# Convolution LayerNorm on VectorE, deferred steps in a woven stream, an early bias table and w2 in 22 loads: one encoder layer on eight cores

## The chip, the cores and the metric

The kernel runs on the 8 cores of one Trainium2 chip, one batch element to a core, with no traffic between cores. The metric is the device time of the slowest core in microseconds (us). The program gives each of a core's five engines a list of its own: PE (matmul), VectorE (DVE in the profile), ScalarE (ACT), GpSimd (POOL) and SP, which here only issues DMAs. In the trace of the kernel before, an instruction that waits holds up what stands behind it in its list: VectorE stood 29.2 us before the copy L423, and the eviction L322, listed after it, came only at 84.3 us. Some executions fall into a second, slower state, in which the cores of a die show a lower granted clock: in the changed kernel's run of 1262.65 us one die shows 0.818 to 0.832 (1252.7 to 1261.1 us), the other 0.973 to 0.978 (1091.8 to 1100.5 us). The medians quoted are those of fast runs alone. Ratios are the mean time of one kernel's fast runs over that of the other's fast runs of the same rounds, so they are not quite the ratio of the medians.

## The reference, cut to what matters

```python
proj = x @ w_in            # conv GLU input | q | k | v | memory q | three branch gates
y_conv = conformer_conv(glu_in, ...)        # GLU -> depthwise conv, width 31 -> LayerNorm -> swish -> projection
y_attn = windowed_gqa(q, k, v, rel_bias, sink) @ w_attn_out     # +-128 tokens, bias by relative position
y_mem  = memory_attention(q_mem, mem, w_mem_kv) @ w_mem_out
gates  = sigmoid(gate_logits + b_gate)
merged = gates[0] * y_conv + gates[1] * y_attn + gates[2] * y_mem
x = layer_norm(ALPHA * x + merged @ w_o, ln1_g, ln1_b)
gate, up = split(x @ w_ffn_in)
return layer_norm(ALPHA * x + (silu(gate) * up) @ w_ffn_out, ln2_g, ln2_b)
```

A core has 2048 tokens of width 1024; the convolution has 512 channels, the FFN 2816.

## The kernel before

The program is one stream per engine. "Main" work (projections) is interleaved with "side" work (convolution, window attention, memory attention) by weight:

```python
def weave(mains, sides):
    ...
    for w, f in mains:
        f()
        mc += w
        while sides and sc + sides[0][0] / 2 <= stot * mc / mt:
            sw, sf = sides.pop(0)
            sf()
            sc += sw
```

The convolution is cut into 16 groups: 4 blocks of 512 tokens by 4 sets of 128 channels. The program's matmuls read each group's input shifted by 0 to 3 tokens and laid out over the partitions. SP makes such a window with 16 small transfers, into one of three buffers:

```python
for j in range(4):
    for r in range(4):
        lo = 32 + 512 * k - 15 + r
        uq_tok[i] = dma(sp, UQ[r3][j][32 * r:32 * r + 32, 0:540],
                        U0[32 * j:32 * j + 32, c, lo:lo + 540], uq_slot[r3], deps)
```

The LayerNorm and swish that end a block run mostly on GpSimd, each step issued as soon as the program reaches it:

```python
def fin(c):
    t_z1 = pool.run(... cvs[c] * rstdb ...)
    ...
    t_th = act.run(... tanh(scale * cvs[c] + bias) ...)
    t_z2 = pool.run(... cvs[c] * gamma/2 + beta/2 ...)
    t_sT[k, c] = dve.run(... (th2[r] + 1) * cvs[c] ...)
```

The bias table of the window attention is made between the first projections, goes to HBM and comes back reversed in three SP loads. The FFN's first weights are cast once into a cache in HBM (`w_bf_cache`, 22 tiles) and read back four times. Its second weights, w2, come in two large loads when the FFN starts.

The softmax here doesn't subtract the row's maximum and nothing guards it: scores larger than these inputs give would overflow.

Of the kernel before, what the change touches and what calls it, by code (L numbers as in the profile page):

```python
# [11 lines left out]
D = 1024  # L12
# [78 lines left out]
def _build(plan):  # L91
# [162 lines left out]
    geb = V(149, [8, 512])  # L254
    Brev = V(155.75, [128, 3, 8, 128])

# [37 lines left out]
    t_pads = pool.run(lambda: nc.gpsimd.memset(U0[:, :, T + 32:UW], 0.0))  # L294
    t_wq = load(wq, w_q_d)
    t_wkv = load(wkv, w_kv_d)
    t_wqm = load(wqm, w_qm_d)
    t_memt = load(memT, memt_d)
    t_wmk = [load(wmk[:, i], w_mkv_d[:, i]) for i in range(2)]
    load_xt(2)  # L300
    load_xt(3)
    t_vones = pool.run(lambda: nc.gpsimd.memset(vaug[:, :, :, 64:65], 1.0))
# [12 lines left out]

    ev = {"i": 0}

    def evac(dst, src, deps):
        ev["i"] += 1
        if ev["i"] % 2:  # L320
            return act.run(lambda: nc.scalar.copy(dst, src), deps)  # L321
        return dve.run(lambda: nc.vector.tensor_copy(dst, src), deps)  # L322
# [13 lines left out]
    def g_gate(k, c):  # L336
        b, tk = group8(lambda kc: wglu[:, c, 1, kc, :], lambda kc: xT[:, k, kc, :], k, [t_glu[c]])
        r = gst["i"] % 3
        gst["i"] += 1
        t = act.run(lambda: nc.scalar.activation(th2[r], ps[:, b, :], AF.Tanh, scale=0.5), [tk, th_free[r]])  # L340
        banks.release(b, t)
        gpend[k, c] = (r, t)
# [58 lines left out]
    def setup_bias():  # L401
        b, dd = banks.alloc(1)
        t_g = mm(ps[0:8, b, :], rb33[:], oh, True, True, [t_small, dd], inc=True)
        t_b0 = act.run(lambda: nc.scalar.activation(ge, ps[0:8, b, :], AF.Exp), [t_g])
        banks.release(b, t_b0)
        t_b1 = dve.run(lambda: nc.vector.tensor_tensor(out=geb, in0=ge, in1=rv, op=ALU.mult), [t_b0, t_small])
        btab["st"] = load(gexp_d.ap(), geb, [t_b1], sp)
        s_mt = new_slot("mt")
        for kb in range(3):
            btab["rev"] = dma(sp, Brev[:, kb, :, :], bass.AP(gexp_d, kb * 128, [[1, 128], [512, 8], [1, 128]]),  # L410
                              s_mt, [btab["st"]])

# [7 lines left out]
    def setup_rev():  # L420
        for kb in range(3):
            src = bass.AP(Brev.tensor, Brev[:, kb, 0, 127:128].offset, [[Brev.ap[0][0], 128], [128, 8], [-1, 128]])
            btab["t"] = dve.run(lambda: nc.vector.tensor_copy(expB[:, kb, :, :], src), [btab["rev"]])  # L423

    uq_slot = [new_slot("uq") for _ in range(3)]
# [35 lines left out]
    def conv_steps(k):  # L461
# [3 lines left out]
        def conv_c(c):  # L465
# [13 lines left out]
            banks.release(b, S["sq", c])  # L479
            S["h", c] = pool.run(lambda: nc.gpsimd.tensor_copy(cvh[c], cvs[c]), [S["cv", c], cst["h"][c]])  # L480

        def stats():
            b, dd = banks.alloc(2)
            for c in range(4):
                t_a = mm(ps[:, b, :], ones_bf[:], cvh[c], c == 0, c == 3, [S["h", c], t_onesb, dd if c == 0 else None],
                         inc=(c == 3))
            for c in range(4):
                t_b = mm(ps[:, b + 1, :], ones_bf[:], sqb[c], c == 0, c == 3, [S["sq", c]], inc=(c == 3))
            cst["h"] = [[t_a]] * 4
            cst["q"] = [[t_b]] * 4  # L490
            S["mean"] = dve.run(lambda: nc.vector.tensor_scalar(
                out=meanb, in0=ps[:, b, :], scalar1=1.0 / 512, scalar2=None, op0=ALU.mult), [t_a, cst["mean"]])
            t_m2 = pool.run(lambda: nc.gpsimd.tensor_tensor(out=rstdb, in0=meanb, in1=meanb, op=ALU.mult),
                            [S["mean"], cst["rstd"]])
            t_var = dve.run(lambda: nc.vector.scalar_tensor_tensor(
                out=rstdb, in0=ps[:, b + 1, :], scalar=1.0 / 512, in1=rstdb, op0=ALU.mult, op1=ALU.subtract), [t_b, t_m2])
            banks.release(b, t_var, 2)
            S["sd"] = act.run(lambda: nc.scalar.activation(rstdb, rstdb, AF.Sqrt, bias=eps_t[:, 0:1]), [t_var, t_eps])

        def recip(i):  # L500
            S["rs"] = dve.run(lambda: nc.vector.reciprocal(rstdb[:, 128 * i:128 * i + 128], rstdb[:, 128 * i:128 * i + 128]),  # L501
                              [S["sd"]])
            S["z0", i] = pool.run(lambda: nc.gpsimd.tensor_tensor(out=cvs[i], in0=cvs[i], in1=meanb, op=ALU.subtract),
                                  [S["mean"], S["h", i]])
            if i == 3:
                cst["mean"] = [S["z0", 3]]

        def fin(c):
            t_z1 = pool.run(lambda: nc.gpsimd.tensor_tensor(out=cvs[c], in0=cvs[c], in1=rstdb, op=ALU.mult),  # L509
                            [S["rs"], S["z0", c]])  # L510
            if c == 3:
                cst["rstd"] = [t_z1]
            r = gst["i"] % 3
            gst["i"] += 1
            t_th = act.run(lambda: nc.scalar.activation(  # L515
                th2[r], cvs[c], AF.Tanh, bias=cvec[:, 8 + c:9 + c], scale=cvec[:, 4 + c:5 + c]),
                [t_z1, t_cvec, th_free[r]])
            t_z2 = pool.run(lambda: nc.gpsimd.tensor_scalar(  # L518
                out=cvs[c], in0=cvs[c], scalar1=cvec[:, 4 + c:5 + c], scalar2=cvec[:, 8 + c:9 + c],
                op0=ALU.mult, op1=ALU.add), [t_th])  # L520
            t_sT[k, c] = dve.run(lambda: nc.vector.scalar_tensor_tensor(  # L521
                out=U0[:, c, 512 * k:512 * k + 512], in0=th2[r], scalar=1.0, in1=cvs[c],
                op0=ALU.add, op1=ALU.mult), [t_z2, t_th])
            th_free[r] = [t_sT[k, c]]
            cst["cv"][c] = [t_sT[k, c]]

        for c in range(4):
            steps.append((1.7, lambda c=c: conv_c(c)))
        steps.append((0.1, lambda: None))
        steps.append((1.7, stats))  # L530
        for i in range(4):
            steps.append((0.4, lambda i=i: recip(i)))
        for c in range(4):
            steps.append((0.4, lambda c=c: fin(c)))
        return steps

# [5 lines left out]
    def w_S(n, kb):  # L542
# [4 lines left out]
        for g in range(2):  # L547
# [8 lines left out]
        banks.release(b, t_p, 2)  # L556
        t_b = dve.run(lambda: nc.vector.tensor_tensor(  # L557
            out=flat, in0=flat, in1=expB[:, kb, :, :].rearrange("p a b -> p (a b)"), op=ALU.mult), [t_p])
        wst.setdefault(("S", n), []).append((kblk, rp, t_b))

# [209 lines left out]
    def weave(mains, sides):  # L770
# [4 lines left out]
        for w, f in mains:  # L775
            f()
            mc += w
            while sides and sc + sides[0][0] / 2 <= stot * mc / mt:
                sw, sf = sides.pop(0)
                sf()  # L780
                sc += sw
        for sw, sf in sides:
            sf()

    def g_list(k, cs=range(4)):
# [14 lines left out]
    def cat(ls):  # L800
# [5 lines left out]

    weave(g_list(0, [0]) + [run(setup_bias)] + g_list(0, [1]) + [run(setup_cw)] + g_list(1, [0, 1]) +
          g_list(0, [2]) + g_list(1, [2]) + g_list(0, [3]) + g_list(1, [3]), [])
# [17 lines left out]
    load_wos(1, [])  # L826
    weave(c1[6:] + c_main(0, 2), merge_lists([cat(M[12:18]), cat(W[12:18])]))
    banks.merge()

# [5 lines left out]
    x1b = [V(183.75 + 2 * i, [128, D]) for i in range(3)]  # L835
    w2 = V(115.75, [128, 22, D])
    actT = V(44, [128, 22, 512])
    sgf = [V(40 + 2 * i, [128, 512], F32) for i in range(2)]
# [24 lines left out]
    cache_w1(4)  # L863
    w1_tok = {}
    w1_free = [[dp2_done], [dp2_done], [], []]
    w1_slot = [new_slot("w1") for _ in range(4)]
# [14 lines left out]
    for i in range(3):  # L881
        load_w1(i)
    x1b_free = [[], [], []]

# [89 lines left out]
    s_out = [new_slot("out") for _ in range(2)]  # L974
    s_w2 = new_slot("w2")
    e_state = {"sgi": 0, "oi": 0}

    def e_start():
        dep = pe.tok()
        dma(pool, w2[:, 0:11, :], w_f2_d[:, 0:11, :], s_w2, [dep])  # L980
        e_state["w2"] = dma(pool, w2[:, 11:22, :], w_f2_d[:, 11:22, :], s_w2)
        e_state["dep"] = dep
# [25 lines left out]
    def e_step(si):  # L1008
# [3 lines left out]
        if jp == 10:  # L1012
            for tbl in range(4):
                tb = Q * 4 + tbl
                bO, dO = banks.alloc(2)
                for half in range(2):
                    for j in range(22):
                        tk = mm(ps[:, bO + half, :], actT[:, j, tbl * 128:(tbl + 1) * 128],
                                w2[:, j, half * 512:(half + 1) * 512], j == 0, j == 21,
                                [dO, e_state["w2"], e_state["a"]] if (half == 0 and j == 0) else (),  # L1020
                                inc=(half == 1 and j == 21))
# [21 lines left out]
    for tb in range(17):  # L1043
# [20 lines left out]
        if tb >= 7:  # L1064
            e_step(tb - 7)
    for r in range(2):
        ost_free[r] = [x1b_free]
# [68 lines left out]
```

## Time and profile before

| | before |
|---|---|
| median | 1151.3 us (1149.9 to 1152.3) |
| PE busy | 1018.6 us, 88% |
| woven stretch ends (next phase's x loads issued) | 386.1 us |
| first double step of the FFN | 650.9 us |
| last output block of the FFN starts | 1102.7 us |

The lines themselves are in the prediction. They are to be read so: PE is the engine that sets the time, so look for the stretches in which it stands still, then ask which wait ends last in each. One view is not in the prediction, PE's timeline where the FFN starts. The columns are start, length, what, and in brackets the idle time before it with what ended it:

```profile
650.89 7.07 PE L221 MATMUL ps<-arena 128*128 128x512 bf16 x32
...
658.24 7.07 PE L221 MATMUL ps<-arena 128*128 128x512 bf16 x32
...
679.17 5.06 PE L221 MATMUL ps<-arena 128*128 128x512 bf16 x16 [13.41 <-DMA arena<-w_bf_cache]
692.79 5.08 PE L221 MATMUL ps<-arena 128*128 128x512 bf16 x16 [8.56 <-DMA arena<-w_bf_cache]
697.70 0.61 PE L960 MATMUL ps<-ident_bf,arena 128*128 128x128 bf16 x8
```

Two double steps of 32 matmuls run 7.35 us apart; the third is broken into two halves that wait for weights.

### The profile page before, as it was taken

To read this page: it belongs to the slowest core of one execution; us is meant where nothing else is said; L and a number is where in the kernel's file an instruction comes from. 1 tells how busy PE (TensorE), PEld (TensorE's weight loads), DVE (VectorE), ACT (ScalarE), POOL (GpSimd) and SP (SyncE) were. 2 spreads that over 40 slices of the span, in tenths; PEclk is the share of its full clock that TensorE was granted. 3 is DMA by queue.
4 is the path that set the end of the run, shared out by engine and by line. 5 is a ranking of instruction groups with operands and counts; after the bars stand their busy time and mean duration, and the time that the engine had idled before them with its cause. 6 is when DMAs were issued, how large, how long until landed. Compare 5 with 4: busy or idle time off the path is not lost.

```text
span 1151.2 us, 15714 instructions; the slowest of 8 cores (1139.8 to 1151.2 us)
## 1 busy us (share of the span) xinstructions
PE 1018.6 (88%) x5662; PEld 467.4 (41%) x5662; DVE 408.5 (35%) x732; ACT 356.2 (31%) x507; POOL 181.2 (16%) x203
## 2 busy tenths in 40 slices
PE   4919999587848999999999939999999999999996
PEld 1404443233324444444444414444444444444442
DVE  1204354526445422222236814424212421242124
ACT  1104444444434222222213737612111211121111
POOL 3000024524251343433310000000000000000000
PEclk9969999798879999999999979999999999999998
DMA  9981111354004598784044394422442244224401
GB/s 138 161 149 47 32 48 33 73 112 76 22 1 83 88 167 121 115 132 74 1 125 168 53 183 162 144 103 90 162 157 69 87 165 157 68 89 163 146 5 70
DMA packets 39515, 116.22 MB, mean 101 GB/s; under 512 B 10368, under 2 KB 18696, under 8 KB 37936
## 3 DMA queue, kind: packets, MB, share of 16 engines
q0 software_dynamic: 8064, 48.76, 24.3%
q1 hardware_dynamic: 31376, 66.46, 18.6%
q8 instruction: 47, 0.77, 0.3%
q14 instruction: 28, 0.23, 0.1%
HBM read 138.32 MB, written 19.93 MB: 137 GB/s over the span
## 4 chain that ended last, share of the span: by engine, by line
PE 76%; DMA 5%; DVE 4%; ACT 4%; SPq 3%; issue 3%; another core or an unknown queue 3%; POOL 2%; DVEq 0%; ACTq 0%; POOLq 0%
PE ps L221 75%; SPq L138 3%; DMA arena<-w_bf_cache 3%; DMA arena<-xt 1%; POOL arena L509 1%; ACT arena L555 1%; DMA arena<-arena 1%; DVE arena L929 1%; DVE arena L501 1%; ACT arena L887 1%; POOL arena L518 0%; ACT arena L515 0%; ACT arena L968 0%; DVE arena L908 0%
## 5 line engine op out<-in xcount | busy, mean ns | idle before, releaser
L221 PE MATMUL ps<-arena 128*128 128x512 bf16 (+5 forms) x5372 | 999.0, 366 | 87.6 <-DVE arena L322 23.2
L221 PEld LDWEIGHTS ps<-arena 128*128 128x128 bf16 (+2 forms) x5372 | 448.5, 99 | 619.2 <-issue 154.1
L1002 DVE TENSOR_TENSOR arena<-ps,arena 128x512 bf16<-128x512 f32 x88 | 60.6, 691 | 226.6 <-PE ps L221 192.8
L734 DVE SCALAR_TENSOR_TENSOR arena<-arena,ps 128x512 f32<-128x512 f32 x96 | 65.8, 686 | 152.1 <-PE ps L221 150.0
L713 ACT ACTIVATE arena<-ps,bgate_sb 128x512 f32<-128x512 f32 x96 | 65.9, 687 | 173.7 <-PE ps L221 173.6
L1000 ACT ACTIVATE arena<-ps 128x512 f32<-128x512 f32 x88 | 51.5, 597 | 192.4 <-PE ps L221 192.2
L138 POOL DMA_DIRECT2D out<-arena x16 | 8.5, 534 | 488.5 <-DVE arena L910 488.5
L887 ACT ACTIVATE arena<-arena 128x1024 bf16<-128x1024 f32 (+1 forms) x32 | 33.8, 1057 | 140.4 <-DVE arena L1023 133.2
L741 POOL TENSOR_TENSOR arena<-arena 128x512 f32<-128x512 f32 x32 | 41.1, 1284 | 137.9 <-DVE arena L734 137.9
L557 DVE TENSOR_TENSOR arena<-arena 128x1024 bf16<-128x1024 bf16 x46 | 32.8, 714 | 62.4 <-ACT arena L555 62.3
L555 ACT ACTIVATE arena<-ps 128x1024 bf16<-128x1024 f32 x46 | 46.6, 1021 | 12.6 <-PE ps L221 12.5
L746 POOL TENSOR_TENSOR arena<-arena 128x512 bf16<-128x512 f32 x32 | 40.9, 1277 | 51.8 <-DVE arena L734 51.8
L1023 DVE SCALAR_TENSOR_TENSOR arena<-arena,ps 128x1024 f32<-128x1024 f32 x16 | 19.5, 1221 | 66.8 <-PE ps L221 66.8
L910 DVE SCALAR_TENSOR_TENSOR arena<-arena,mvt 128x1024 f32<-128x1024 f32 x32 | 41.1, 1285 | 4.0 <-DVE arena L908 0.5
L908 DVE SCALAR_TENSOR_TENSOR arena<-arena,mvt 128x1024 f32<-128x1024 f32 x32 | 41.0, 1281 | 2.3 <-DVE mvt L904 0.7
L480 POOL CAST arena<-arena 128x512 bf16<-128x512 f32 x16 | 10.6, 661 | 179.6 <-ACT arena L475 179.6
L521 DVE SCALAR_TENSOR_TENSOR arena<-arena 128x512 bf16<-128x512 f32 x16 | 21.1, 1320 | 32.4 <-POOL arena L518 30.9
L321 ACT CAST arena<-ps 128x512 bf16<-128x512 f32 (+1 forms) x24 | 13.6, 566 | 60.4 <-PE ps L221 60.4
L515 ACT ACTIVATE arena<-arena,cvec_sb 128x512 f32<-128x512 f32 x16 | 13.0, 813 | 47.8 <-POOL arena L509 47.8
L929 DVE SCALAR_TENSOR_TENSOR arena<-arena,ps 128x1024 f32<-128x1024 f32 x16 | 19.4, 1212 | 18.3 <-PE ps L221 18.3
L591 PE MATMUL ps<-ident_bf,arena 128*128 128x128 bf16 x64 | 7.9, 227 | 20.2 <-DVE arena L576 20.1
L509 POOL TENSOR_TENSOR arena<-arena 128x512 f32<-128x512 f32 x16 | 20.2, 1262 | 18.7 <-DVE arena L501 18.7
(82 smaller groups left out, 377.2 us busy)
## 6 DMA issues: line engine op xcount, KB each, us to landing
arena<-w_bf_cache SPq DMA_DIRECT2D x88, 512.0 KB, 3.8
arena<-arena SPq DMA_DIRECT2D x256, 33.8 KB, 1.9
arena<-x SPq DMA_DIRECT2D x16, 512.0 KB, 12.4
out<-arena POOLq DMA_DIRECT2D x16, 512.0 KB, 3.0
w_bf_cache<-w_f POOLq DMA_DIRECT2D x3, 2560.0 KB, 48.2
arena<-w_g POOLq DMA_DIRECT2D x12, 512.0 KB, 11.5
arena<-w_f POOLq DMA_DIRECT2D x2, 2816.0 KB, 32.4
arena<-xt POOLq DMA_DIRECT2D x8, 512.0 KB, 41.2
```

Of the source, the lines that this page charges most:

```text
L138: e.eng.dma_start(out=out, in_=in_).then_inc(slot.sem, 16)
L221: return pe.run(lambda: nc.tensor.matmul(out, lhsT, rhs, start=start, stop=stop), deps, inc)
L555: t_p = act.run(lambda: nc.scalar.activation(flat, bank2(b), AF.Exp, scale=0.125), [tk, PTw_free[rp], btab["t"]])
L713: t = act.run(lambda: nc.scalar.activation(gb[r], ps[:, bk, :], AF.Tanh, bias=bgate[:, b * 8 + dc:b * 8 + dc + 1], scale=0.5), [tk, gb_fre ...
L734: t_y = dve.run(lambda: nc.vector.scalar_tensor_tensor(out=gb[r], in0=gb[r], scalar=1.0, in1=ps[:, bk, :], op0=ALU.add, op1=ALU.mult), [tk ...
L741: c_state["s"] = pool.run(lambda: nc.gpsimd.tensor_tensor(out=gb[r0], in0=gb[r0], in1=gb[r], op=ALU.add), [c_state["y", 0], t_y])
L746: t_mg[dp, tt, dci] = pool.run(lambda: nc.gpsimd.tensor_tensor(out=merged[dp][:, dci, tt * 512:(tt + 1) * 512], in0=gb[r0], in1=gb[r], op= ...
L887: return act.run(lambda: nc.scalar.activation(junk, buf, AF.Square, accum_out=st[:, 1:2]), deps)
L908: te = dve.run(lambda: nc.vector.scalar_tensor_tensor(out=buf, in0=buf, scalar=mv[:, 0:1], in1=tabs[:, 0, :], op0=ALU.subtract, op1=ALU.mu ...
L910: return dve.run(lambda: nc.vector.scalar_tensor_tensor(out=dst, in0=buf, scalar=mv[:, 2:3], in1=tabs[:, 1, :], op0=ALU.mult, op1=ALU.add) ...
L1000: t_s = act.run(lambda: nc.scalar.activation(sgf[sr], ps[:, bG, :], AF.Silu), [tG, sg_free[sr]])
L1002: t_a = dve.run(lambda: nc.vector.tensor_tensor(out=actT[:, j, :], in0=ps[:, bU, :], in1=sgf[sr], op=ALU.mult), [tU, t_s, e_state["dep"]])
```

## The change

Its intent is to let no engine stand in order before a result that another engine has only begun to make. It has three parts that touch different stretches, cut here to the core.

Bias table: made first, loaded once, in runs of 384 elements, on GpSimd's queue.

```diff
-        s_mt = new_slot("mt")
-        for kb in range(3):
-            btab["rev"] = dma(sp, Brev[:, kb, :, :], bass.AP(gexp_d, kb * 128, [[1, 128], [512, 8], [1, 128]]), ...)
+        btab["rev"] = load(Brev, bass.AP(gexp_d, 0, [[1, 128], [512, 8], [1, 384]]), [btab["st"]])
...
+    setup_bias()
+    t_wq = load(wq, w_q_d)        # these loads stood before the set-up of the table
```

Woven stretch: the LayerNorm's steps go to VectorE; a step that needs another engine's fresh result is deferred by one slot of the weave; evictions (copies of matmul results out of PSUM) go 2 to 1 to ScalarE instead of 1 to 1.

```diff
+    def later(n, fn):
+        due.append([n, fn])
...
-            S["h", c] = pool.run(lambda: nc.gpsimd.tensor_copy(cvh[c], cvs[c]), ...)
+            def hcopy():
+                S["h", c] = dve.run(lambda: nc.vector.tensor_copy(cvh[c], cvs[c]), ...)
+            later(1, hcopy)
...
-            t_z1 = pool.run(...)
+            t_z1 = dve.run(...)
+            t_z2 = dve.run(...)             # affine step now before tanh
+            def fin_th():
+                t_th = act.run(... tanh ...)
+                def fin_s():
+                    t_sT[k, c] = dve.run(...)
+                later(1, fin_s)
+            later(1, fin_th)
...
-        t_b = dve.run(... window attention: exp * bias table ...)
+        def mult(): t_b = dve.run(...)
+        later(1, mult)
```

w2: 22 tiles, nine loaded when the branch phase ends and two after each of the next steps.

```diff
-        dma(pool, w2[:, 0:11, :], w_f2_d[:, 0:11, :], s_w2, [dep])
-        e_state["w2"] = dma(pool, w2[:, 11:22, :], w_f2_d[:, 11:22, :], s_w2)
...
+    load_w2(0, 9, [c_done, t_mg[3, 3, 1]])
...
+            load_w2(9 + 2 * (tb - 7), min(22, 11 + 2 * (tb - 7)), pe.tok())
```

More of the change, by code (lines that the diff above doesn't have):

```diff
@@ L254, in _build @@
     geb = V(149, [8, 512])
-    Brev = V(155.75, [128, 3, 8, 128])
+    Brev = V(155.75, [128, 8, 384])
     s_small = new_slot("small")
@@ L294, in _build @@
     t_pads = pool.run(lambda: nc.gpsimd.memset(U0[:, :, T + 32:UW], 0.0))
-    t_wq = load(wq, w_q_d)
-    t_wkv = load(wkv, w_kv_d)
-    t_wqm = load(wqm, w_qm_d)
-    t_memt = load(memT, memt_d)
-    t_wmk = [load(wmk[:, i], w_mkv_d[:, i]) for i in range(2)]
-    load_xt(2)
-    load_xt(3)
     t_vones = pool.run(lambda: nc.gpsimd.memset(vaug[:, :, :, 64:65], 1.0))
@@ L316, in _build, with tick @@
     ev = {"i": 0}
+    due = []
+    def later(n, fn):
+        due.append([n, fn])
+    def tick():
+        ready = []
+        for d in due:
+            d[0] -= 1
+            if d[0] <= 0:
+                ready.append(d)
+        for d in ready:
+            due.remove(d)
+        for d in ready:
+            d[1]()
     def evac(dst, src, deps):
         ev["i"] += 1
-        if ev["i"] % 2:
+        if ev["i"] % 3:
             return act.run(lambda: nc.scalar.copy(dst, src), deps)
@@ L339, in g_gate @@
         gst["i"] += 1
+        assert th_free[r] is not None
         t = act.run(lambda: nc.scalar.activation(th2[r], ps[:, b, :], AF.Tanh, scale=0.5), [tk, th_free[r]])
+        th_free[r] = None
         banks.release(b, t)
@@ L407, in setup_bias @@
         btab["st"] = load(gexp_d.ap(), geb, [t_b1], sp)
-        s_mt = new_slot("mt")
-        for kb in range(3):
-            btab["rev"] = dma(sp, Brev[:, kb, :, :], bass.AP(gexp_d, kb * 128, [[1, 128], [512, 8], [1, 128]]),
-                              s_mt, [btab["st"]])
+        btab["rev"] = load(Brev, bass.AP(gexp_d, 0, [[1, 128], [512, 8], [1, 384]]), [btab["st"]])
     def setup_cw():
@@ L421, in setup_rev @@
         for kb in range(3):
-            src = bass.AP(Brev.tensor, Brev[:, kb, 0, 127:128].offset, [[Brev.ap[0][0], 128], [128, 8], [-1, 128]])
+            src = bass.AP(Brev.tensor, Brev[:, 0, kb * 128 + 127:kb * 128 + 128].offset,
+                          [[Brev.ap[0][0], 128], [384, 8], [-1, 128]])
             btab["t"] = dve.run(lambda: nc.vector.tensor_copy(expB[:, kb, :, :], src), [btab["rev"]])
+    setup_bias()
+    t_wq = load(wq, w_q_d)
+    t_wkv = load(wkv, w_kv_d)
+    t_wqm = load(wqm, w_qm_d)
+    t_memt = load(memT, memt_d)
+    t_wmk = [load(wmk[:, i], w_mkv_d[:, i]) for i in range(2)]
+    load_xt(2)
+    load_xt(3)
     uq_slot = [new_slot("uq") for _ in range(3)]
@@ L479, in conv_c @@
             banks.release(b, S["sq", c])
-            S["h", c] = pool.run(lambda: nc.gpsimd.tensor_copy(cvh[c], cvs[c]), [S["cv", c], cst["h"][c]])
+            def hcopy():
+                S["h", c] = dve.run(lambda: nc.vector.tensor_copy(cvh[c], cvs[c]), [S["cv", c], cst["h"][c]])
+            later(1, hcopy)
         def stats():
@@ L492, in stats, with sqrt @@
                 out=meanb, in0=ps[:, b, :], scalar1=1.0 / 512, scalar2=None, op0=ALU.mult), [t_a, cst["mean"]])
-            t_m2 = pool.run(lambda: nc.gpsimd.tensor_tensor(out=rstdb, in0=meanb, in1=meanb, op=ALU.mult),
-                            [S["mean"], cst["rstd"]])
-            t_var = dve.run(lambda: nc.vector.scalar_tensor_tensor(
+            t_m2 = dve.run(lambda: nc.vector.tensor_tensor(out=rstdb, in0=meanb, in1=meanb, op=ALU.mult),
+                           [S["mean"], cst["rstd"]])
+            S["var"] = dve.run(lambda: nc.vector.scalar_tensor_tensor(
                 out=rstdb, in0=ps[:, b + 1, :], scalar=1.0 / 512, in1=rstdb, op0=ALU.mult, op1=ALU.subtract), [t_b, t_m2])
-            banks.release(b, t_var, 2)
-            S["sd"] = act.run(lambda: nc.scalar.activation(rstdb, rstdb, AF.Sqrt, bias=eps_t[:, 0:1]), [t_var, t_eps])
+            banks.release(b, S["var"], 2)
+        def sqrt():
+            S["sd"] = act.run(lambda: nc.scalar.activation(rstdb, rstdb, AF.Sqrt, bias=eps_t[:, 0:1]), [S["var"], t_eps])
         def recip(i):
@@ L502, in recip, with z0 @@
                               [S["sd"]])
-            S["z0", i] = pool.run(lambda: nc.gpsimd.tensor_tensor(out=cvs[i], in0=cvs[i], in1=meanb, op=ALU.subtract),
-                                  [S["mean"], S["h", i]])
-            if i == 3:
-                cst["mean"] = [S["z0", 3]]
+        def z0(i):
+            S["z0", i] = dve.run(lambda: nc.vector.tensor_tensor(out=cvs[i], in0=cvs[i], in1=meanb, op=ALU.subtract),
+                                 [S["mean"], S["h", i]])
         def fin(c):
-            t_z1 = pool.run(lambda: nc.gpsimd.tensor_tensor(out=cvs[c], in0=cvs[c], in1=rstdb, op=ALU.mult),
-                            [S["rs"], S["z0", c]])
@@ L511, in fin @@
-            if c == 3:
-                cst["rstd"] = [t_z1]
-            r = gst["i"] % 3
-            gst["i"] += 1
-            t_th = act.run(lambda: nc.scalar.activation(
-                th2[r], cvs[c], AF.Tanh, bias=cvec[:, 8 + c:9 + c], scale=cvec[:, 4 + c:5 + c]),
-                [t_z1, t_cvec, th_free[r]])
-            t_z2 = pool.run(lambda: nc.gpsimd.tensor_scalar(
-                out=cvs[c], in0=cvs[c], scalar1=cvec[:, 4 + c:5 + c], scalar2=cvec[:, 8 + c:9 + c],
-                op0=ALU.mult, op1=ALU.add), [t_th])
@@ L521, in fin @@
-            t_sT[k, c] = dve.run(lambda: nc.vector.scalar_tensor_tensor(
-                out=U0[:, c, 512 * k:512 * k + 512], in0=th2[r], scalar=1.0, in1=cvs[c],
-                op0=ALU.add, op1=ALU.mult), [t_z2, t_th])
-            th_free[r] = [t_sT[k, c]]
-            cst["cv"][c] = [t_sT[k, c]]
+            t_z1 = dve.run(lambda: nc.vector.tensor_tensor(out=cvs[c], in0=cvs[c], in1=rstdb, op=ALU.mult),
+                           [S["rs"], S["z0", c]])
+            cst["rstd"] = [t_z1]
+            t_z2 = dve.run(lambda: nc.vector.tensor_scalar(
+                out=cvs[c], in0=cvs[c], scalar1=cvec[:, 4 + c:5 + c], scalar2=cvec[:, 8 + c:9 + c],
+                op0=ALU.mult, op1=ALU.add), [t_z1, t_cvec])
@@ new lines, in fin_th @@
+            def fin_th():
+                r = gst["i"] % 3
+                gst["i"] += 1
+                assert th_free[r] is not None
+                t_th = act.run(lambda: nc.scalar.activation(th2[r], cvs[c], AF.Tanh), [t_z2, th_free[r]])
+                def fin_s():
+                    t_sT[k, c] = dve.run(lambda: nc.vector.scalar_tensor_tensor(
+                        out=U0[:, c, 512 * k:512 * k + 512], in0=th2[r], scalar=1.0, in1=cvs[c],
+                        op0=ALU.add, op1=ALU.mult), [t_z2, t_th])
+                    th_free[r] = [t_sT[k, c]]
+                    cst["cv"][c] = [t_sT[k, c]]
+                th_free[r] = None
+                later(1, fin_s)
@@ L530, in conv_steps @@
         steps.append((1.7, stats))
+        steps.append((0.4, lambda: z0(0)))
+        steps.append((0.4, lambda: (sqrt(), z0(1))))
         for i in range(4):
-            steps.append((0.4, lambda i=i: recip(i)))
+            steps.append((0.4, (lambda i=i: (recip(i), z0(2 + i))) if i < 2 else (lambda i=i: recip(i))))
         for c in range(4):
             steps.append((0.4, lambda c=c: fin(c)))
+        steps.append((0.4, lambda: None))
+        steps.append((0.4, lambda: None))
         return steps
@@ L556, in w_S, with mult @@
         banks.release(b, t_p, 2)
-        t_b = dve.run(lambda: nc.vector.tensor_tensor(
-            out=flat, in0=flat, in1=expB[:, kb, :, :].rearrange("p a b -> p (a b)"), op=ALU.mult), [t_p])
-        wst.setdefault(("S", n), []).append((kblk, rp, t_b))
+        def mult():
+            t_b = dve.run(lambda: nc.vector.tensor_tensor(
+                out=flat, in0=flat, in1=expB[:, kb, :, :].rearrange("p a b -> p (a b)"), op=ALU.mult), [t_p])
+            wst.setdefault(("S", n), []).append((kblk, rp, t_b))
+        later(1, mult)
     def w_V(n, g):
@@ L776, in weave @@
             f()
+            tick()
             mc += w
@@ L780, in weave @@
                 sf()
+                tick()
                 sc += sw
@@ L783, in weave @@
             sf()
+            tick()
     def g_list(k, cs=range(4)):
@@ L805, in _build @@
     CV = [conv_steps(k) for k in range(4)]
-    weave(g_list(0, [0]) + [run(setup_bias)] + g_list(0, [1]) + [run(setup_cw)] + g_list(1, [0, 1]) +
+    weave(g_list(0, [0]) + g_list(0, [1]) + [run(setup_cw)] + g_list(1, [0, 1]) +
           g_list(0, [2]) + g_list(1, [2]) + g_list(0, [3]) + g_list(1, [3]), [])
@@ L827, in _build @@
     weave(c1[6:] + c_main(0, 2), merge_lists([cat(M[12:18]), cat(W[12:18])]))
+    while due:
+        tick()
     banks.merge()
@@ L835, in _build @@
     x1b = [V(183.75 + 2 * i, [128, D]) for i in range(3)]
-    w2 = V(115.75, [128, 22, D])
-    actT = V(44, [128, 22, 512])
+    w2 = [V(o, [128, D]) for o in (48, 50, 52, 156.5, 44, 46, 62, 64, 191.75, 54, 56, 58, 60,
+                                   140.5, 142.5, 144.5, 146.5, 148.5, 150.5, 152.5, 154.5, 138.5)]
+    actT = V(116.5, [128, 22, 512])
     sgf = [V(40 + 2 * i, [128, 512], F32) for i in range(2)]
@@ L864, in _build, with load_w2 @@
     w1_tok = {}
+    s_w2 = new_slot("w2")
+    e_state = {"sgi": 0, "oi": 0}
+    def load_w2(lo, hi, dep):
+        for j in range(lo, hi):
+            e_state["w2"] = dma(pool, w2[j], w_f2_d[:, j, :], s_w2, [dep])
     w1_free = [[dp2_done], [dp2_done], [], []]
@@ L974, in _build @@
     s_out = [new_slot("out") for _ in range(2)]
-    s_w2 = new_slot("w2")
-    e_state = {"sgi": 0, "oi": 0}
     def e_start():
         dep = pe.tok()
-        dma(pool, w2[:, 0:11, :], w_f2_d[:, 0:11, :], s_w2, [dep])
-        e_state["w2"] = dma(pool, w2[:, 11:22, :], w_f2_d[:, 11:22, :], s_w2)
         e_state["dep"] = dep
@@ L1018, in e_step @@
                         tk = mm(ps[:, bO + half, :], actT[:, j, tbl * 128:(tbl + 1) * 128],
-                                w2[:, j, half * 512:(half + 1) * 512], j == 0, j == 21,
+                                w2[j][:, half * 512:(half + 1) * 512], j == 0, j == 21,
                                 [dO, e_state["w2"], e_state["a"]] if (half == 0 and j == 0) else (),
```

## The prediction

> **What bounds the kernel now.** I read the cores first: all eight lie between 1139.8 and 1151.2 us at a granted clock of 0.952 to 0.959, so this is the fast state and no core stands out. Then the page, then the busy time by stretches, then the waits, then the chain.
>
> ```profile
> span 1151.2 us, 15714 instructions; the slowest of 8 cores (1139.8 to 1151.2 us)
> PE 1018.6 (88%) x5662; PEld 467.4 (41%) x5662; DVE 408.5 (35%) x732; ACT 356.2 (31%) x507; POOL 181.2 (16%) x203
> ```
>
> PE is busy 88% of the span and no other engine is over 35%. So time can be won only where PE stands still, and the question is where its 133 us of standing still lie. Busy time by stretches answers that:
>
> ```profile
> 61.00:85.00 24.00, 1.00 (x5) 0.27 (x3) 1.68 (x5) 0.59 (x1) 0.00 (x0) 0.57 0.88 152
> 85.00:121.00 36.00, 35.41 (x256) 17.40 (x257) 16.42 (x38) 14.74 (x19) 0.00 (x0) 0.96 0.15 40
> ...
> 183.00:193.50 10.50, 10.50 (x105) 4.72 (x104) 4.39 (x7) 5.66 (x9) 2.98 (x4) 1.00 0.20 48
> 193.50:221.00 27.50, 17.88 (x140) 7.98 (x138) 11.58 (x13) 11.46 (x16) 14.49 (x15) 0.88 0.21 54
> ...
> 299.00:316.00 17.00, 11.73 (x70) 5.37 (x68) 6.60 (x14) 7.41 (x8) 5.98 (x5) 0.83 0.01 1
> 316.00:343.00 27.00, 12.19 (x81) 4.98 (x80) 11.43 (x19) 8.54 (x11) 12.96 (x12) 0.75 0.00 1
> 343.00:386.00 43.00, 38.44 (x307) 19.95 (x306) 26.58 (x68) 20.01 (x25) 9.52 (x9) 0.91 0.32 56
> ```
>
> After the stretch come its length, then busy time (count) of PE, PE's weight loads, VectorE, ScalarE and GpSimd, the clock, the DMA share and GB/s. From 386 to 616 us PE is busy without a break, and from 693 to 1141 for 443.75 of 448 us. So the losses are four: the first 17 us, one hole at 61 to 85, a loose stretch from 150 to 386 where convolution and both attentions are woven into the projections, and one at 660 to 693 (11.03 of 33 us busy). The waits name three of them:
>
> ```profile
> DVE arena L521 <- POOL arena L518: 30.9, 13, 5.4
> DVE arena L423 <- DMA arena<-gexp_scratch: 29.2, 1, 29.2
> ...
> PE ps L221 <- DVE arena L322: 23.2, 1, 23.2
> ...
> PE ps L221 <- DMA arena<-w_bf_cache: 22.0, 2, 13.4
> PE ps L591 <- DVE arena L576: 20.1, 8, 9.4
> ```
>
> The numbers are us in total, times, longest. The first hole is a chain: VectorE stands 29.2 us before L423, the copy of the reversed bias table, waiting for its DMA. An eviction (L322) sits behind it, the PSUM banks are not given back, and PE stands 23.2 us. The fourth line is the first FFN weights, which arrive late. The first and the last belong to the loose stretch.
>
> That stretch has one more limit. In the timeline the SP queue issues 16 small transfers for each of the 16 shifted convolution windows ("units"), at about 0.64 us each, so 10.2 us a unit. From 182.92 to 292.7 us it sends units 7 to 15, and apart from one gap of 6.4 us it never rests: 103 us of issuing, 11.5 us a unit, with some slowed by other traffic. The chain of waits agrees:
>
> ```profile
> by line: PE ps L221 45.1%; SPq L138 14.6%; issue 9.1%; POOL arena L509 4.1%; ACT arena L555 3.7%; DMA arena<-arena 3.5%; DVE arena L501 2.5%; POOL arena L518 1.9%; ACT arena L515 1.9%; ACT arena L713 1.2%; ACT arena L630 1.1%; PE ps L591 1.
> ```
>
> This is the chain between 120 and 390 us. SP's issuing holds 14.6% of it, more than all GpSimd lines together. The change does not touch it.
>
> [...] the three table loads (256-byte runs, 3072 of them) took 44.1 to 52.9 us to land while the DMA share was 0.96 to 1.05, and landed just as the queue of cast loads ran dry at 82 us. [...] L521 has a minimum of 692 ns, a median of 1602 and a maximum of 1610, and runs beside GpSimd work. [...] 0.57 in the hole, and eight matmuls 0.43 us apart after it.
>
> **The change, part by part.**
>
> *Bias table early.* The table is made before all projections and loaded as one transfer of 1024 runs of 768 bytes. The small inputs land at 16.7 us (ScalarE waits until then), exp and product add 3, the store 5 as now, so the load starts near 25 instead of 29. Now each DMA engine moves 192 table packets in 53 us, 0.28 us each. A third of them is 64, some 18 us. It lands near 45, and VectorE needs it at about 54. The 23.2 us vanish, and so does the cold start after it (8 matmuls x 0.2 = 1.6 us). Against it, PE must now first wait for the small inputs (16.7 instead of 13.5 us), about 1.5 us. The weights needed next land in time: now at 50 us (memory queries), 61 to 68 (memory keys and values) and 82 (last x); PE wants them at about 70, 84 and 100. **Gain 23 us.**
>
> *Convolution LayerNorm from GpSimd to VectorE, chains split over slots.* Moved for each of 4 blocks: 4 casts, 1 square, 4 subtractions, 4 products, 4 affine steps. Nine tensor-tensor at 0.69 us[...] are 9.6 us a block, 38 us in all. VectorE gets back about 0.9 us on each of 16 L521 (14 us) and 11 evictions that go to ScalarE (7 us): net +17 on the 142 us it is busy between 85 and 386. It does not become the bound. What PE gains differs by part:
> - 150 to 183 us: PE busy 28.7 of 33. Gain 4.
> - 183 to 299: bound by SP. The same nine units need the same 103 us; only the gap of 6.4 us can go. Gain 5, not the 25 us that PE stands still there.
> - 299 to 386: no convolution loads remain. PE is busy 62.4 of 87 us, some 3 of it on a slow clock, and waits for GpSimd chains of 3.1 us a channel group (L509, L515, L518) and evictions behind them. I choose two thirds of the 24.6 us. **Gain 16.**
>
> Together **25 us**.
>
> *w2 in 22 pieces.* Now both halves start at 650.7 us and fill the DMA (share 1.02) for 33 us; the double-sized w1 steps, 7.35 us apart otherwise, start at 650.89 and for the fifth at 698.31 instead of 680.3. Loss 18 us. In the new kernel nine pieces go at about 590 (old clock), with the x loads, of which the last land at 616; from 616 to 650 the DMA share is 0.05, so there is room. The other 13 go two per step: 0.5 MB at the 174 GB/s of this queue (48.76 MB in 24.3% of the span) is 3.0 us, w1's 1 MB at 310 GB/s (66.46 MB in 18.6%) 3.4 us: 6.4 of 7.35 us. It fits, barely. **Gain 17 us.**
>
> Sum: 23 + 25 + 17 = 65, so 1151.3 - 65 = **1086 us**.
>
> **The rivals.**
> - *SP's issuing takes back the gain of the weave.* I have this in the sum. If it is tighter, because the convolution loads meet weight loads that GpSimd, now without arithmetic, issues sooner (the w1 cache starts at 277.7 us now, behind GpSimd's chain), each unit takes 12 to 13 us: time about 1097. For it: the landing of 9.5 us on the chain at 225 us, where weights come in.
> - *SP is no bound,* as issuing runs at its undisturbed 10.2 us a unit and PE fills in: 9 x 1.3 = 12 us less, and all idle after it, 8 less: about 1066.
> - *VectorE becomes the bound* in the two densest blocks: by my count 22 us of work in some 26 us. Evictions then come late: 8 to 12 us more, about 1097. Against it: the split takes its waits away.
> - *The w1 wait stays* as 13 small waits: 1100.
>
> **Range and chances.** The bias part is sure within 3 us, w2 within 6, the weave within 15. Combined I say 1066 to 1112. Slower or within 2% (over 1128) would need both the weave and the w2 part to fail: 4% and 1%.
>
> **What would show it.** Right: no VectorE wait for the bias load, PE without a hole at 61 to 85; SP in the chain of waits still, with nine units over 95 to 105 us; GpSimd without arithmetic before the branch outputs, L521's successor at 0.69 us; PE's wait for the w1 cache under 5 us; matmul stretches after as dense as now. Wrong: if PE is busy throughout the woven stretch, SP was no bound; if VectorE shows long busy runs with PE waiting on evictions, it has become one; if the x loads of the second phase or w1 come late, the pieces of w2 are in the way.

One term is the cost on VectorE of eight of the 17 moved steps of a block, the 4 casts and 4 affine steps. The 9.6 us a block, 38 us in all and the net of 17 include it. The nine others make 6.2 us of the 9.6, at the 0.69 us that the trace shows for another VectorE step over 512 float32 elements a partition (L1002, 691 ns). The 0.57 that stands alone is the clock granted from 61 to 85 us. That L521 takes 692 ns at the least and 1602 at the median, beside GpSimd's work, is measured; why is not shown.

## The result, and the profile after

The changed kernel took **1103.2 us** (fast runs 1101.3 to 1103.5) against 1151.3; the ratio is 0.9578 (95% interval 0.9556 to 0.9601). The prediction of 1086 was 17 us too low, within its range. In the profiled run all eight cores lie between 1092.8 and 1099.7 us. First the head of the page:

```profile
span 1099.7 us, 15676 instructions; the slowest of 8 cores (1092.8 to 1099.7 us)
PE 1008.7 (92%) x5662; PEld 466.1 (42%) x5662; DVE 434.6 (40%) x789; ACT 359.4 (33%) x518; POOL 124.9 (11%) x156
```

VectorE has 57 more instructions and 26 us more, GpSimd 56 us less; PE is now busy 92%. The stretches show which holes closed (columns as in the prediction):

```profile
54.00:85.00 31.00, 31.00 (x208) 15.20 (x206) 9.91 (x20) 10.96 (x16) 0.00 (x0) 1.00 0.88 173
...
197.00:225.00 28.00, 13.75 (x128) 6.25 (x128) 8.41 (x20) 10.23 (x15) 1.06 (x2) 0.76 0.59 106
225.00:252.00 27.00, 16.82 (x138) 9.36 (x139) 7.21 (x15) 8.94 (x11) 0.00 (x0) 0.74 0.43 102
252.00:270.00 18.00, 9.73 (x78) 3.88 (x77) 15.63 (x28) 6.90 (x11) 0.00 (x0) 0.72 0.03 9
...
290.00:360.00 70.00, 59.54 (x476) 29.98 (x476) 55.82 (x115) 37.80 (x47) 13.82 (x13) 0.95 0.18 35
...
640.00:668.00 28.00, 28.00 (x149) 13.43 (x148) 16.04 (x31) 26.40 (x35) 3.79 (x8) 1.00 0.96 216
```

PE is busy throughout 54 to 85 and 640 to 668 us, where the two large holes were. It is busy only 40.3 of the 73 us from 197 to 270. PE's waits, longest in total first, say on what:

```profile
PE ps L221 <- DMA arena<-arena: 22.4, 3, 19.5
PE ps L221 <- DMA esink<-sinkp: 16.8, 1, 16.8
PE ps L625 <- DVE arena L610: 11.3, 4, 6.4
PE ps L221 <- ACT arena L664: 9.1, 5, 5.8
```

Of the three waits of over 20 us in the kernel before, two are gone, and the one for the last step of a window attention (L610 here, L576 there) fell from 20.1 to 11.3. A wait for the convolution windows (`arena<-arena`), 3.0 us there, is now 22.4, of which one is 19.5. The second line is the start: PE waits 16.8 us for the small inputs, where its first wait was 13.5 us before, as the prediction allowed for.

To see where the time went I used marks that exist in both kernels: ScalarE's first read of convolution groups 0, 4 and 15, the issue of the x loads that ends the woven stretch, and the two starts in the FFN from the table above.

| stretch, us | before | after | gained | predicted |
|---|---|---|---|---|
| start to group 0 | 125.5 | 102.1 | 23.3 | 23 |
| group 0 to 4 | 59.5 | 60.6 | -1.2 | 4 |
| group 4 to 15 | 112.4 | 125.6 | -13.2 | 5 |
| group 15 to end of woven stretch | 88.7 | 71.7 | 17.0 | 16 |
| from there to first FFN double step | 264.8 | 264.5 | 0.3 | 0 |
| first double step to last output block | 451.8 | 426.6 | 25.2 | 17 |

Three of six terms are off, and they partly cancel: groups 0 to 4 by 5 us, groups 4 to 15 by 18, w2 by 8 the other way.

In the convolution stretch three pieces of the chain of waits tell the story (start, length, what):

```profile
216.46 0.59 SPq L138
217.09 16.17 DMA arena<-arena
...
233.40 6.97 PE ps L221 x66
```

SP issued the last transfer of group 11's window at 217.1, having issued since 162.8 with no pause of over 0.4 us; it landed 16.2 us later, where the median is 1.9; only then could PE go on. GpSimd's timeline shows what started just before:

```profile
212.70 0.53 POOL L138 DMA_DIRECT2D arena<-w_out  x1 [23.68 <-PE ps L221]
213.22 0.54 POOL L138 DMA_DIRECT2D w_bf_cache<-w_f  x1
```

These are a weight load and the first copy into the w1 cache (`w_bf_cache`); the copy takes 19.2 us to land, until 232.4. In the kernel before, the copy went out at 277.7, because GpSimd's arithmetic stood ahead of it (its last affine step, L518, ran from 277.0 us until then).

### The profile page after: what moved, and what is told of

The parts are those of the page before. It is cut to its first block, busy times and chain, and to the rows that moved or that the text cites. A ratio compares the mean times of both kernels' runs of the same rounds, so it can differ in the third digit from the quotient of the medians.

```text
span 1099.7 us, 15676 instructions; the slowest of 8 cores (1092.8 to 1099.7 us)
## 1 busy us (share of the span) xinstructions
PE 1008.7 (92%) x5662; PEld 466.1 (42%) x5662; DVE 434.6 (40%) x789; ACT 359.4 (33%) x518; POOL 124.9 (11%) x156
## 3 DMA queue, kind: packets, MB, share of 16 engines
q1 hardware_dynamic: 28256, 65.67, 19.3%
## 4 chain that ended last, share of the span: by engine, by line
PE 83%; SPq 5%; DVE 5%; DMA 3%; ACT 3%; issue 2%; DVEq 0%; POOL 0%; ACTq 0%; POOLq 0%
PE ps L221 81%; SPq L138 5%; DMA arena<-arena 1%; DMA esink<-sinkp 1%; DVE arena L977 1%; ACT arena L935 1%; DVE arena L524 1%; DVE arena L532 1%; ACT arena L664 0%; ACT arena L1016 0%; PE ps L625 0%; PE ps L1008 0%; DVE arena L535 0%; DVE arena L956 0%; DVE arena L546 0%
## 5 line engine op out<-in xcount | busy, mean ns | idle before, releaser
L221 PE MATMUL ps<-arena 128*128 128x512 bf16 (+5 forms) x5372 | 989.3, 365 | 41.8 <-DMA arena<-arena 22.4
L1046 DVE TENSOR_TENSOR arena<-ps,arena 128x512 bf16<-128x512 f32 x88 | 60.6, 691 | 201.0 <-PE ps L221 180.3
L775 POOL TENSOR_TENSOR arena<-arena 128x512 f32<-128x512 f32 x32 | 40.4, 1263 | 199.3 <-DVE arena L768 189.8
L1067 DVE SCALAR_TENSOR_TENSOR arena<-arena,ps 128x1024 f32<-128x1024 f32 x16 | 19.5, 1221 | 67.2 <-PE ps L221 67.2
L590 DVE TENSOR_TENSOR arena<-arena 128x1024 bf16<-128x1024 bf16 x46 | 35.0, 760 | 14.8 <-ACT arena L587 14.8
L330 ACT CAST arena<-ps 128x512 bf16<-128x512 f32 (+1 forms) x29 | 16.5, 571 | 36.1 <-PE ps L221 36.1
L500 DVE CAST arena<-arena 128x512 bf16<-128x512 f32 x16 | 6.8, 426 | 53.9 <-ACT arena L493 53.9
L493 ACT ACTIVATE arena<-ps,cvec_sb 128x512 f32<-128x512 f32 x16 | 11.0, 688 | 47.4 <-PE ps L221 47.3
L138 POOL DMA_DIRECT2D arena<-w_g x12 | 6.5, 554 | 154.6 <-PE ps L221 154.6
L138 POOL DMA_DIRECT2D arena<-w_f x22 | 11.7, 548 | 100.9 <-PE ps L1008 100.3
## 6 DMA issues: line engine op xcount, KB each, us to landing
arena<-arena SPq DMA_DIRECT2D x256, 33.8 KB, 1.9
```

Of the source, the lines that this page charges most:

```text
L138: e.eng.dma_start(out=out, in_=in_).then_inc(slot.sem, 16)
L221: return pe.run(lambda: nc.tensor.matmul(out, lhsT, rhs, start=start, stop=stop), deps, inc)
L775: c_state["s"] = pool.run(lambda: nc.gpsimd.tensor_tensor(out=gb[r0], in0=gb[r0], in1=gb[r], op=ALU.add), [c_state["y", 0], t_y])
L1046: t_a = dve.run(lambda: nc.vector.tensor_tensor(out=actT[:, j, :], in0=ps[:, bU, :], in1=sgf[sr], op=ALU.mult), [tU, t_s, e_state["dep"]])
```

## The experiments

Twelve kernels were run, and all gave a correct result. The theory: **(A)** the weave is worth about what I predicted, but SP's 16 issues a window take it back, and the w1 copy, now early, worsens that. The rivals: **(B)** SP only fills time that VectorE's dense LayerNorm chain costs anyway; **(C)** one of the other parts earns less than its stretch shows, and the weave more.

### The three parts alone

The edits are the three parts of the diff above, each put on the kernel before by itself.

> The kernel before with the bias part alone. If the three parts simply add, this gains what the first convolution group moved forward in the changed kernel (125.5 to 102.1 us): 23 us, so 1128. If the shift is eaten later, because the SP queue bounds the woven stretch whatever comes before it, the end of that stretch (386 us before) moves by less than 23 and the time is 1135 to 1145.

> The kernel before with w2 in pieces alone. By the prediction's sum 17 us (1134); by the traces of the two kernels the stretch from the first FFN step to the last output block is 25.2 us shorter (fourth double step at 698.15 instead of 672.9), so 1126. No rival for the cause: PE's 22 us of waiting for the w1 cache should be gone.

> The changed kernel without its bias and w2 parts: the LayerNorm on VectorE and the split chains alone. Theory A (the weave gains 17 us after the last convolution group and gives 13 to 14 back before it, to the SP queue and the traffic in its way): 1146 to 1150. Theory B (the weave is worth the predicted 25 us and something in the bias part took it back): 1126.

| | median, us | ratio to before (95%) |
|---|---|---|
| bias table | 1132.7 | 0.9825 (0.9802 to 0.9849) |
| w2 in pieces | 1126.1 | 0.9769 (0.9754 to 0.9784) |
| weave | 1149.8 | 0.9969 (0.9952 to 0.9985) |

The losses of ratio are 1.75, 2.31 and 0.31%, together 4.37; the three parts in one kernel gave 4.22. So they add up, and rival C falls: the weave alone is worth 3.6 us (0.31% of 1152). In the weave-only kernel the copy is issued at 236 us, and group 11 follows group 10 by 28.0 us (234.55 to 262.56), so the collision comes with this part and not with the bias table. The bias table alone fell between its two expectations: group 0 came 22.7 us earlier, the end of the woven stretch 17.9.

### The w1 copy later

```diff
-    cache_w1(3)                 # after the fourth woven stage
     c1 = c_main(0, 1)
...
+    cache_w1(3)                 # after the last one
     banks.merge()
```

> The changed kernel with the first copy into the w1 cache (3 of 22 tiles) issued at the end of the woven stretch instead of at 213 us. Theory A (this copy stands in the way of the convolution windows of group 11, which land 16 us after their issue while PE waits 19.5 us): that wait falls to 4 to 8 us, time 1088 to 1093. Theory B (SP's issuing alone sets the pace, the copy only fills the wait): the group comes no earlier, time 1100 to 1104.

It took 1090.3 us, ratio 0.9457 (0.9441 to 0.9473), 1.2% or 14 us below the changed kernel. PE's waits for the windows:

```profile
PE ps L221 <- DMA arena<-arena: 10.9, 3, 6.7
```

The longest fell from 19.5 to 6.7 us and groups 4 to 15 took 114.5 us instead of 125.6. So the copy did stand in the way. But 114.5 is still no less than the 112.4 of the kernel before. As the parts add, the kernel before with the other two parts would stand at 1 less 0.0175 and 0.0231, or 0.9594 (worked out, not run). So with the copy out of the way the weave is worth 0.0137, some 16 us. The stretch after group 15 accounts for about that: 72.1 us instead of 88.7.

### Four transfers a window instead of sixteen

Each projected piece is copied once to HBM, and the windows are read from there. One transfer now fills all four channel sets of a shift. The runs stay 1080 bytes long and as many; the count of issues falls from 16 to 4 (and one for the copy). The source moves too, from SBUF to HBM, and no run separates the two. But a transfer does not land sooner for it, at the median 3.5 us after issue where the small ones took 1.9, while SP, which issued most of the small transfers (33.8 KB each) 0.62 us apart, is done with a window in about 1.7 us instead of 10.

```diff
-        for j in range(4):
-            for r in range(4):
-                uq_tok[i] = dma(sp, UQ[r3][j][32 * r:32 * r + 32, 0:540], U0[32 * j:32 * j + 32, c, lo:lo + 540], ...)
+        for r in range(4):
+            uq_tok[i] = dma(sp, UQ4[r3][32 * r:32 * r + 32, :, 0:540],
+                            bass.AP(ud_d, c * UW + lo, [[4 * UW, 32], [32 * 4 * UW, 4], [1, 540]]), ...)
```

It was run on the kernel with the late copy, on the kernel before, and on the changed kernel as it is.

> The kernel with the late w1 cache copy (1090), but each convolution window loaded by 4 transfers from a copy in HBM (written by one transfer per projected group) instead of 16 within SBUF; same number of runs of 1080 bytes. If SP's issuing (16 x 0.64 us a unit) bounds the stretch: PE's 10.9 us of waiting for the windows vanish and the time is 1076 to 1082. If VectorE's chain sets the pace there: 1086 to 1091.

> The kernel before with the same 4 transfers a unit and nothing else. If SP bounded it too (103 of 110 us of issuing between groups 4 and 15): 1136 to 1145. If GpSimd's chains and the engines behind them were the bound and SP only filled their time: 1148 to 1153.

> The changed kernel with 4 transfers a convolution window, the w1 cache copy left where the change puts it (213 us). If the copy hurt only because SP had no time in hand (issues late, so the windows queue behind it): windows are issued before it and the time is 1076 to 1080, as with the late copy. If the copy holds up the packets whoever issues them: PE still waits 8 to 16 us for a window and the time is 1084 to 1092.

| | median, us | ratio to before (95%) | groups 4 to 15, us |
|---|---|---|---|
| late copy, 4 transfers | 1076.8 | 0.9348 (0.9326 to 0.9370) | 100.9 |
| before, 4 transfers | 1149.8 | 0.9982 (0.9960 to 1.0003) | 106.3 |
| changed kernel, 4 transfers, copy early | 1076.9 | 0.9351 (0.9330 to 0.9373) | 100.7 |

With 4 transfers no wait of PE for a window is left in the first and third. Rival B falls for the changed kernel: its VectorE work is the same, and 26 us went with the way the windows are loaded (0.9578 to 0.9351). The chain of waits over the woven stretch, first of the changed kernel, then of the late copy with 4 transfers:

```profile
by line: PE ps L221 49.9%; SPq L138 18.9%; DMA arena<-arena 6.1%; issue 5.7%; DVE arena L524 2.3%; DVE arena L532 2.3%; ACT arena L664 1.9%; DVE arena L535 1.6%; PE ps L625 1.5%; DVE arena L546 1.3%; ACT arena L587 1.2%; DVE arena L528 0.9%
```

```profile
by line: PE ps L222 66.9%; issue 5.6%; DVE arena L532 4.0%; DVE arena L540 3.6%; DVE arena L543 2.5%; ACT arena L672 2.1%; DVE arena L554 2.1%; DVE arena L536 1.6%; PE ps L633 1.6%; ACT arena L595 1.3%; PE ps L706 1.3%; ACT arena L551 0.8%;
```

SP's issues and the landings, a quarter of the first chain, do not show among the lines of the second. What is left beside PE is VectorE's LayerNorm.

The third row also bounds what the copy's fault was. With 4 transfers the early copy costs nothing (1076.9 against 1076.8). There the copy goes out at 209.8 us, after the windows of groups 11 to 13 (198.6, 201.9 and 208.1), and the one that follows it, at 212.4, is not needed before 250. In the changed kernel group 11's own issues ran from 206.1 to 217.7. So it hurts where SP is late enough for a window that PE needs next to meet it.

The second row was my miss. On the kernel before, the same edit is worth 2.1 us, with an interval that touches zero. Groups 4 to 15 shrink by 6 us, no more (by the profiles the woven stretch ends 5.0 us earlier, and the FFN, where the wait for w1 is still there, takes 2.3 longer), and the chain between 120 and 390 us there now reads:

```profile
by line: PE ps L222 52.3%; issue 10.3%; POOL arena L517 7.4%; ACT arena L523 4.0%; POOL arena L526 3.7%; ACT arena L563 3.7%; DVE arena L509 3.2%; ACT arena L721 1.3%; PE ps L672 1.2%; PE ps L599 1.0%; DVE arena L584 0.8%; POOL arena L501 0
```

L517 and L526 are GpSimd's product and affine step, L523 the tanh between them. So between groups 4 and 15 the kernel before had two limits of nearly the same length side by side: SP's issues and GpSimd's chain. Taking SP's away alone gives 6 us there, taking GpSimd's alone nothing (114.5 us with the late copy, against 112.4 before and 114.9 with the bias table alone), and both together 11.5. The weave on top of 4 transfers can be worked out, as the parts add: 0.9982 less 0.0175 and 0.0231 for the other parts is 0.9576, and 0.9351 was measured; the difference of 0.0225 is 26 us. With 16 transfers the same weave is worth 3.6 us, or some 16 with the copy out of the way: about half of what was missing was the copy, the rest SP.

### Splitting and moving apart

The weave's two main parts were each undone in the kernel with the late copy (1090.3, ratio 0.9457).

```diff
     def later(n, fn):
-        due.append([n, fn])
+        fn()
```

> The kernel with the late w1 cache copy (1090), LayerNorm on VectorE, but every deferred step issued at once. If the splitting earns the gain after the last convolution group: PE again waits behind in-order VectorE and ScalarE, 1098 to 1108. If it earns nothing: 1089 to 1092.

It took 1109.8 us, ratio 0.9636 (0.9619 to 0.9653): the splitting is worth 1.8%, 21 us. PE's waits behind VectorE show how:

```profile
PE ps L625 <- DVE arena L610: 21.7, 9, 9.8
```

Against 11.2 us in 4 waits with the splitting, so this line shows half of the loss. L610 is the last VectorE step of a window attention. Without deferral VectorE itself stands still ahead of it: 43.6 us in all before bias products that wait for ScalarE's exponentials (7.8 with the splitting), and 13.6 before the LayerNorm's last product, which waits for the tanh (2.0). In the two longest waits, of 9.8 and 7.3 us, it is mostly the latter.

```diff
-                S["h", c] = dve.run(lambda: nc.vector.tensor_copy(cvh[c], cvs[c]), ...)
+                S["h", c] = pool.run(lambda: nc.gpsimd.tensor_copy(cvh[c], cvs[c]), ...)
     (likewise the square, the subtraction, the product and the affine step)
```

> The kernel with the late w1 cache copy (1090), chains split, but the casts, squares, subtractions, products and affine steps of the convolution LayerNorm back on GpSimd. If the move to VectorE is what helps (1.26 us a product on GpSimd, about 0.61 on VectorE[...]): 1096 to 1104. If VectorE's dense runs before the waits of 5.8 and 6.4 us are the worse evil: 1080 to 1089.

It took 1093.1 us, ratio 0.9493 (0.9472 to 0.9514): the move is worth some 0.36%, 4 us, which lies between the two expectations, and the two intervals all but touch. Set beside the 0.9594 worked out above for a kernel with neither, the move alone (0.9636) loses some 5 us, the splitting alone (0.9493) wins 12, and both (0.9457) win 16, each within some 4 us by the intervals. So nearly all of the weave's worth is the order of issue, not the engine. Both kernels keep the evictions at 2 to 1 and the affine step before the tanh; what these two are worth was not tested.

### A version faster than both

In the kernel with late copy and 4 transfers PE still waits 6.4, 5.8 and 5.1 us behind dense VectorE runs. Two edits were tried: the casts and the subtraction of the mean back on GpSimd, which is busy 5.2 of the 129 us from 161 to 290 in the changed kernel (chain still split), and the last four steps of a block spaced wider in the weave.

```diff
-        steps.append((0.4, lambda c=c: fin(c)))
+        steps.append((1.0, lambda c=c: fin(c)))
```

> The kernel with late copy and 4 transfers a window (1076.8), with only the casts and the subtraction of the mean back on GpSimd, which is idle there: 8 of 17 moved instructions a block leave VectorE, in its dense runs. If VectorE's density is what is left (PE waits 5.8, 5.1 and 6.4 us behind it): 1066 to 1073. If GpSimd's slower steps[...] give it back: 1075 to 1079.

> The kernel with late copy and 4 transfers a window (1076.8), the four final LayerNorm steps of a block spaced wider (weight 1.0 instead of 0.4 in the weave), so that VectorE's work is less bunched before the attention step that waits. If bunching is the cause of the waits that are left: 1066 to 1073. If the work itself is too much for VectorE there: 1075 to 1080.

> Late copy, 4 transfers a window, casts and mean subtraction on GpSimd and the four final LayerNorm steps spaced wider: both edits of the last two runs (fast runs near 1073 and 1075) together. If they free the same VectorE runs: 1071 to 1074. If they add: 1068 to 1071.

The first had one fast run of four, 1073.3 us; in the others some cores ran at a lower clock (0.958 to 0.959, in the slowest also 0.854 to 0.871, against 0.982 to 0.985 on the rest). Where a die was undisturbed in them, its cores took 1070.2 to 1072.3 us, against 1071.4 to 1076.1 in the fast runs of the kernel with late copy and 4 transfers, so it is probably faster by 2 to 3 us, though its waits of 6.4 and 4.9 us stayed. The second took 1075.1 us (0.9336, 0.9315 to 0.9357), not clearly different from 0.9348: the long waits broke up into shorter ones behind ScalarE (9.6 us in 5 waits and 5.0 in 5). Both together took **1068.3 us**, ratio 0.9258 (0.9243 to 0.9274), 3.3% below the changed kernel (0.9258 against 0.9578). That is more than the single edits promise (3.5 and 1.6 us). The marks put it before group 15: from group 0 to there the profiles show 161.6 us with neither edit, 158.0 and 158.5 with one, 152.6 with both. Why the two help each other stays open; the time fits the expectation of two edits that add, and not that of two that free the same time.

## Why the prediction was right or wrong

- **Bound and four losses.** Right: PE sets the time, and what was won was won in its holes.
- **Bias table, 23 us.** Right in size: 23.3 us to group 0, and 1.75% (20 us) as a change alone. Its route was not as I worked it out. I scaled the old load's 53 us down to a third of the runs and let it land near 45 us after 18; that was an estimate. It stands in GpSimd's own queue, ahead of the other loads, which wait 19.3 us for it, and lands 10.0 us after its issue at 26.6. The waiting weights still came in time. As a change alone it lost some 5 of its 23 us again by the end of the woven stretch.
- **Weave before group 4, 4 us.** Wrong by 5: it lost 1.2. PE's wait of 5.8 us up to 156 us (`ACT arena L664`) took the place of two of about 2 us; the chain leads through ScalarE's tanh back to VectorE's LayerNorm.
- **"183 to 299: bound by SP ... Gain 5".** This is the step that failed. I took the units' 103 us of issuing as given and asked only for the gap. The issuing held, at 100 us for the nine units. But the gap grew from 6.4 to 16.3 us (253.4 to 269.6) instead of going, and a landing of 16.2 us came into the path: groups 4 to 15 got 13.2 us longer. The copy into the w1 cache had moved from 277.7 to 213.2 us and met the windows. I had named that among the rivals ("SP's issuing takes back the gain of the weave", 1097), with the right cause, though as 12 to 13 us of issuing a unit where it was 11.1, and left it out of the sum. The late copy gives 13 us of the 17 back: 1090.
- **SP as the bound of the kernel before.** Half wrong. SP's share of the chain there did not mean that the stretch would follow SP: 4 transfers gave 6 us in the stretch and 2 in the time. It was one of two limits of like length. For the changed kernel it is right: loading the windows with 4 transfers won 26 us.
- **After the last group, 16 us.** Right: 17.0. My guess of two thirds of PE's idle time had no working behind it, so this is luck in part. The source was mainly the splitting: from 88.7 us this stretch falls to 81.0 with the move alone, 75.2 with the splitting alone and 72.1 with both. The sum spoke of both as one.
- **Cost of the moved steps, 9.6 us a block.** Near: the product took 684 ns (0.69 estimated), the cast 426 and the affine step 547 at the median, and by the profile's sums the 17 steps took 10.3 us a block. L546, the successor of L521, has a median of 686 ns as said. The net was off: VectorE got 26 us busier, not 17. L521's mean was 1320 ns and only its median 1602, so its successor gave back 10 us and not 14.
- **w2, 17 us.** The term was mis-sized by a miscount: the double step at 698.15 us is the fourth, not the fifth, and would stand at 672.9, so the loss was 25.2 us and not 18. Alone the part gave 2.31%, 27 us. That w1 and the pieces share the DMA without a wait ("fits, barely") was right: the share was 0.96 from 640 to 668 us and PE never waited for w1.
- **VectorE as the bound** did not come about over the stretch in the changed kernel, though the 6.4 us that PE waits for L610 end a dense run of VectorE's LayerNorm there; it is what shows next once SP is relieved.

## What to carry to other kernels

If two engines' work runs side by side and both nearly fill a stretch, removing either can show little (6 us and nothing here, 11.5 for both); test the pair before you call one harmless, and before you call a change worthless. Moving arithmetic off an engine can also move the DMAs that this engine issues behind it (here the copy into the w1 cache, from 277.7 to 213.2 us), so look up what will now start early and whose packets it meets. Most of what a "move" earns may be the order of issue: undoing the deferral by one slot cost 21 us here, undoing the move to the other engine 4.
